# A hybrid RWKV-7 / S5 decoder layer on one core: the instruction order of the whole kernel made by the scheduler's other machine model

## The chip, the cores and the metric

The kernel runs on one core of one Trainium2 chip. The metric is the device time of one execution in microseconds (us), the median of several runs. Engines are named as in the profile: PE is the matrix engine (TensorE), DVE is VectorE, ACT is ScalarE, POOL is GpSimd, and SP is the engine that issues most of the DMA transfers. L172 means line 172 of the kernel. A "gap" of PE is time in which no matmul runs.

## What is computed

One layer of a decoder trunk, float32, 1024 tokens by 1024 channels. The reference, cut to its chain:

```
h = rms_norm(x) ; p = h @ w_in                  # columns: RWKV-7 r,k,v and low-rank parts | S5 input u | two gates
A = rwkv7_branch(p[rwkv columns])               # token shift, decay, delta-rule state, 8 heads of 64
B = s5_branch(p[S5 columns])                    # 32 groups, 64 complex states each, then GELU and a sigmoid GLU
m = sigmoid(gate_A) * (A @ w_A) + sigmoid(gate_B) * (B @ w_B)
x = x + rms_norm(m @ w_out)
z = rms_norm(x) @ w_up ; z = conv_b + sum(conv_w[j] * shift(z, 2 - j) for j in 0..2)
gate, val = split(z) ; x = x + rms_norm((gelu(gate) * val) @ w_down)
```

## The kernel before

**Tiling.** Activations are kept channel by token, in tiles of 128 channels by 512 tokens, so the 1024 tokens are two halves (`th` 0 and 1) and the 1024 channels are eight tiles (`k`). Each matrix product in float32 is made of three matmuls on a high and a low part of each operand: high times high, high times low, low times high (L172 to L174 in `mm3_steps`, L1049 to L1051 in `start`, L1614 to L1616 in `down`). Parts are made by a cast on ACT and a subtraction on DVE: L226/L227 (`split`) and L231/L232 (`split_half`) for activations, L156/L157 (`load_w`) for weights. A weight tile thus costs a load on SP's queue (`wf`, L155), a cast on ACT (`wh`, L156) and a subtraction on DVE (`wl`, L157), and DVE's part of it must be done before the third of its matmuls.

**Stages, in order of time.**

- `start` (L951 to L1061; the first 80 us). The columns of the S5 input, for token half 0 and then half 1. The loop runs over the eight `k`, and inside over four column blocks `b`, each with its own PSUM bank `gm`. Alongside, DVE adds up squares (L989, L991); `root` and `scales` make the norm's factors `rbc` with the reciprocal root `rsy` (L131 to L139). After the last `k` of half 0, `evict` (L1011 to L1020) empties each bank with one DVE multiplication, L1013. Half 1 starts in the same four banks, so its first matmul in bank `b` (L1049) waits for the L1013 of bank `b`. `scaled` (L1006 to L1009) multiplies the input tiles by `rbc` on DVE (L1008) and splits them (L226/L227) for all later products.
- `s5_setup` (from L311). DVE rows on 128x32 tiles, a chain that makes the coefficients of the S5 recurrence (sine, cosine, powers). They are needed by later stages only.
- The input projections of RWKV-7 (`rkv`, L1073 to L1077 make the token shift from the PSUM bank), `rwkv_prep` (L640 to L737: scans L672, products L691 to L696, L704, masks L720, shrinks L736), the inverse and state steps, `rwkv_out` (L901 to L939: norms over a head), the gates (L1147 empties a bank on ACT), the S5 branch (L1166/L1167 load a tile and apply GELU on ACT), L812 (block transposes of S5 data on DVE that the L822 matmuls read).
- The two branch projections and their merge (L1192, L1238, L1275, splits L232), `outproj`, and beside it `mid_norms(0)` for the first half of the tokens, with `post_norm` (L1295 scales, L1296 adds the residual, L259 sums squares).
- The MLP: `first_units` (four tiles of the up projection, convolution L1381/L1383 on DVE), `prep_t` (L1357 to L1368: differences and splits of eight tiles), then `fast_up` (a convolution with fewer products; `fast_weights`, L1408 to L1433, loads two weight tiles `r1` and `r2` of 128x1024 by L1420/L1421), and `down` with the last norm.

**What sets the order.** PE's order is written out: the program runs in a section whose PE order is manual (L1748), and `drive` and `background` (L185 to L223) interleave several generators into it. For DVE, ACT, POOL and SP a scheduler takes the instructions, their dependences and priorities, and a model of the machine, and makes one list for each engine before the kernel is run. Priorities are raised in places: weights (HPW and HPN, 400000 and 500000), the RWKV and norm lanes (HP, HP2, 100000 and 200000, L1932 and L1933). On the chip every engine works through its own list. The few lines of `start` that matter for the first 80 us:

```
for th in range(2):
    ps = [self.gmp() for b in range(4)]
    for k in range(NK):
        for b in range(4):
            ...
            nc.tensor.matmul(ps[b], a, hi, start=k == 0, stop=False)
            ...
            if k == NK - 1:
                evict(th, b, ps[b])
        ...
        if th:
            scaled(0, k)
```

## Time and profile before

| what | us |
|---|---|
| median of 3 runs (1488.82 to 1491.57) | 1489.53 |
| span of the profiled execution | 1491.1 |
| PE busy | 1435.8 |
| DVE busy | 1071.2 |
| ACT busy | 729.8 |
| POOL busy | 58.9 |

The profile is of one execution, whose span is 1.6 us above the median of the runs. Busy times are sums over the whole span; the waits and the order of time are in the views that the prediction shows. In rows of the timeline the columns are: start, duration, engine, line, operation, output and inputs, tile shape, count, and in brackets the idle time of the engine just before and what ended it. In rows of the windows the columns are: stretch, its length, then busy time and count for PE, PE's weight loads, DVE, ACT and POOL, the granted clock of PE (1.00 is full), the share of the DMA engines in use and GB/s.

### The profile page before, as it was taken

The page shows a single profiled execution, that of the slowest core. Times are in us where ns is not written, and L with a number is a line of the kernel's source. Part 1 is how long each engine was busy: PE and PEld are TensorE (multiplying, and loading weights), DVE is VectorE, ACT ScalarE, POOL GpSimd, SP SyncE. Part 2 cuts the span into 40 slices and gives each one's busy share as a digit, 9 for nine tenths or more (in the row PEclk, how much of TensorE's full clock was granted, in tenths as well). Part 3 has the DMA queues.
Part 4 walks back from the last instruction along what each step waited for, and adds up shares of the span by engine and source line. Part 5 has one row for each costly group of instructions (what it writes and reads, how often), then busy time and mean ns, then how long its engine had stood idle before and what let it go on. Part 6 is the DMA issues. An engine that isn't in the chain of part 4 may idle for free. (4 is left out here: it accounts for less than half of the span.)

```text
span 1491.1 us, 24155 instructions
## 1 busy us (share of the span) xinstructions
PE 1435.8 (96%) x9284; PEld 1176.3 (79%) x9284; DVE 1071.2 (72%) x1761; ACT 729.8 (49%) x1167; POOL 58.9 (4%) x116
## 2 busy tenths in 40 slices
PE   7999999999999989899999999999999999999996
PEld 5778888778878778677878877888888887888785
DVE  8977765665325859646597798777777777697677
ACT  7677653443324553633554455444444444443351
POOL 0000000010100110100000000000000000000001
PEclk9999999999999999899999999999999999999998
DMA  6453433633511575733374643222222227934723
GB/s 217 121 194 116 129 94 91 212 113 122 164 59 58 171 226 163 189 109 108 121 222 150 205 127 121 85 85 85 85 85 81 76 70 260 328 125 133 236 83 113
DMA packets 121284, 206.26 MB, mean 138 GB/s; under 512 B 29248, under 2 KB 35520, under 8 KB 121168
## 3 DMA queue, kind: packets, MB, share of 16 engines
q1 hardware_dynamic: 113296, 182.43, 39.2%
q0 software_dynamic: 6144, 19.99, 4.0%
q10 hardware_dynamic: 1728, 2.29, 0.4%
q8 instruction: 73, 1.20, 0.4%
q14 instruction: 43, 0.35, 0.1%
HBM read 150.14 MB, written 52.43 MB: 136 GB/s over the span
## 5 line engine op out<-in xcount | busy, mean ns | idle before, releaser
L172 PE MATMUL gm<-hh,wh 128*128 128x512 f32 x672 | 277.0, 412 | 10.5 <-DVE ev L1192 4.3
L173 PE MATMUL gm<-hl,wh 128*128 128x512 f32 x672 | 265.4, 395 | 0.0
L174 PE MATMUL gm<-hh,wl 128*128 128x512 f32 x672 | 265.2, 395 | 0.0
L156 ACT CAST wh<-wf 128x512 fp32r<-128x512 f32 x171 | 105.6, 619 | 168.3 <-PE gm L173 103.8
L157 DVE TENSOR_TENSOR wl<-wf,wh 128x512 fp32r<-128x512 f32 x171 | 116.9, 686 | 77.6 <-ACT wh L156 77.3
L172 PEld LDWEIGHTS gm<-hh,wh 128*128 128x128 f32 x672 | 127.6, 190 | 42.8 <-issue 5.9
L174 PEld LDWEIGHTS gm<-hh,wl 128*128 128x128 f32 x672 | 128.0, 190 | 28.1
L173 PEld LDWEIGHTS gm<-hl,wh 128*128 128x128 f32 x672 | 128.2, 191 | 24.7 <-issue 1.0
L1615 PE MATMUL d<-xl,wh 128*128 128x512 f32 x308 | 121.4, 394 | 3.5 <-DVE xl L227 3.5
L1614 PE MATMUL d<-xh,wh 128*128 128x512 f32 x308 | 121.4, 394 | 2.1 <-ACT xh L226 2.1
L1616 PE MATMUL d<-xh,wl 128*128 128x512 f32 x308 | 121.2, 393 | 0.0
L1440 PE MATMUL rp<-t,h 128*128 128x512 f32 x216 | 84.4, 391 | 1.6 <-ACT p L1454 1.6
L1442 PE MATMUL rp<-t,l 128*128 128x512 f32 x216 | 84.2, 390 | 0.5 <-DVE l L227 0.5
L1441 PE MATMUL rp<-t,h 128*128 128x512 f32 x216 | 84.1, 389 | 0.0
L1615 PEld LDWEIGHTS d<-xl,wh 128*128 128x128 f32 x308 | 58.6, 190 | 16.5 <-DVE xl L227 4.3
L1614 PEld LDWEIGHTS d<-xh,wh 128*128 128x128 f32 x308 | 58.5, 190 | 14.8 <-ACT xh L226 2.5
L1616 PEld LDWEIGHTS d<-xh,wl 128*128 128x128 f32 x308 | 58.6, 190 | 12.2
L226 ACT CAST h<-r 128x1024 fp32r<-128x1024 f32 x34 | 35.8, 1054 | 61.1 <-PE rp L1441 29.6
L227 DVE TENSOR_TENSOR l<-r,h 128x1024 fp32r<-128x1024 f32 x34 | 41.6, 1224 | 29.2 <-ACT h L226 27.7
L1461 DVE SCALAR_TENSOR_TENSOR y<-zv,vecs,y 128x1023 f32<-128x1023 f32 (+1 forms) x36 | 46.1, 1280 | 8.5 <-ACT y L1459 8.5
L1440 PEld LDWEIGHTS rp<-t,h 128*128 128x128 f32 x216 | 40.5, 188 | 11.2 <-ACT p L1454 2.5
L1454 ACT COPY p<-rp 128x512 f32<-128x512 f32 x54 | 31.0, 574 | 36.5 <-PE rp L1442 36.5
(459 smaller groups left out, 3199.4 us busy)
## 6 DMA issues: line engine op xcount, KB each, us to landing
r<-in_w_up_dram SPq DMA_DIRECT2D x36, 512.0 KB, 3.7
wf<-in_w_in_dram SPq DMA_DIRECT2D x62, 256.0 KB, 3.1
st<-in_w_down_dram SPq DMA_DIRECT2D x55, 256.0 KB, 4.1
st<-ACT SPq DMA_DIRECT2D x44, 256.0 KB, 4.5
wf<-in_w_up_dram SPq DMA_DIRECT2D x36, 256.0 KB, 2.9
ACT<-y POOLq DMA_DIRECT2D x18, 512.0 KB, 2.9
GT<-ev SPq DMA_DIRECT2D x32, 256.0 KB, 2.6
wf<-in_w_br_dram SPq DMA_DIRECT2D x32, 256.0 KB, 2.9
```

Source lines behind the costliest of these rows:

```text
L156: nc.scalar.copy(h[:, :n], f[:, :n])
L157: nc.vector.tensor_tensor(l[:, :n], f[:, :n], h[:, :n].bitcast(F32), ALU.subtract)
L172: mm(ps, a, xh[k], start=k == 0, stop=False)
L173: mm(ps, a, xl[k], start=False, stop=False)
L174: mm(ps, b, xh[k], start=False, stop=k == n - 1)
L1440: mm(ps, wh[:, c], xh, start=first and k == 0, stop=False, skip_group_check=True)
L1441: mm(ps, wh[:, c], xl, start=False, stop=False, skip_group_check=True)
L1442: mm(ps, wl[:, c], xh, start=False, stop=k == 3, skip_group_check=True)
L1461: V.scalar_tensor_tensor(y[:, lag:], z[:, 0:1024 - lag], self.vec(nme, i), y[:, lag:], ALU.mult, ALU.add)
L1614: mm(ps, wh[:, c], xh[:, x], start=start, stop=False, skip_group_check=True)
L1615: mm(ps, wh[:, c], xl[:, x], start=False, stop=False, skip_group_check=True)
L1616: mm(ps, wl[:, c], xh[:, x], start=False, stop=stop, skip_group_check=True)
```

## The change

One line of `build` opens a scheduling block around the whole kernel, with a flag that has the scheduler use its other machine model (a simulation of the timeline) when it makes the lists of the engines:

```
     def build(self):
         tc, nc = self.tc, self.nc
-        with tc.tile_pool(name="const", bufs=1) as self.const, tc.tile_pool(name="small", bufs=1) as self.small, \
+        with tc.block(schedule_with_timeline_sim=True), tc.tile_pool(name="const", bufs=1) as self.const, tc.tile_pool(name="small", bufs=1) as self.small, \
                 tc.tile_pool(name="dram", bufs=1, space=DRAM) as self.dram:
```

The instructions, their tiles and their counts stay the same on every engine, and so does the order of PE's 7448 instructions. What moves is the lists of the others: 1176 of DVE's 1761 rows (by up to 105 places later and 76 earlier), 495 of ACT's, 305 of SP's 688 transfers, 24 of POOL's. The numbers in tile names are higher by one after the change: `gm_346` before is `gm_347` after.

The first place is DVE's list in `start`. `ev` <- `gm` is the L1013 row that empties a bank, `x` the L1008 scaling, `sm`, `pw`, `s5q`, `s5ar` and `s5ai` the small rows of `s5_setup`. Before:

```order
76 L324 TENSOR_SCALAR sm_821<-sm_809 128x32
77 L1008 SCALAR_TENSOR_TENSOR x_198<-x_198,vecs,rbc_482 128x512
78 L1013 TENSOR_TENSOR ev_501<-gm_346,rbc_482 128x512
79 L991 TENSOR_TENSOR sq_540<-sq_540,sq_494 128x512
80 L1013 TENSOR_TENSOR ev_509<-gm_347,rbc_482 128x512
81 L227 TENSOR_TENSOR hl_562<-x_198,hh_561 128x512
82 L1013 TENSOR_TENSOR ev_517<-gm_348,rbc_482 128x512
83 L1008 SCALAR_TENSOR_TENSOR x_199<-x_199,vecs,rbc_482 128x512
84 L1008 SCALAR_TENSOR_TENSOR x_200<-x_200,vecs,rbc_482 128x512
85 L1013 TENSOR_TENSOR ev_525<-gm_349,rbc_482 128x512
```

The same engine after, around the first and the last of the four evictions:

```order
151 L331 TENSOR_TENSOR sm_970<-sm_928,sm_965 128x32
152 L1013 TENSOR_TENSOR ev_502<-gm_347,rbc_483 128x512
153 L1008 SCALAR_TENSOR_TENSOR x_199<-x_199,vecs,rbc_483 128x512
154 L1008 SCALAR_TENSOR_TENSOR x_200<-x_200,vecs,rbc_483 128x512
155 L1008 SCALAR_TENSOR_TENSOR x_201<-x_201,vecs,rbc_483 128x512
156 L1008 SCALAR_TENSOR_TENSOR x_202<-x_202,vecs,rbc_483 128x512
```

```order
184 L439 TENSOR_SCALAR s5w_988<-sm_974 64x32
185 L439 TENSOR_SCALAR s5w_991<-sm_974 64x32
186 L439 TENSOR_SCALAR s5w_988<-sm_980 64x32
187 L439 TENSOR_SCALAR s5w_991<-sm_980 64x32
188 L465 TENSOR_TENSOR s5ar<-pw_1016,pw_1017 128x64
189 L1013 TENSOR_TENSOR ev_526<-gm_350,rbc_483 128x512
```

The four evictions stood in rows 78, 80, 82 and 85, and stand in rows 152, 166, 181 and 189. Ahead of the fourth came 104 rows: 92 small ones, seven splits L227 and five scalings L1008.

The second place is DVE's list beside the output projection, where `hl` <- `et`, `hh` is the low half of a tile (L232) that PE reads next, `mx` are the rows of `post_norm` (L1295, L1296), and `tm` the sums of squares (L259). Before:

```order
1010 L232 SCALAR_TENSOR_TENSOR hl_8312<-et_8288,hh_8311 128x512
1011 L1192 SCALAR_TENSOR_TENSOR et_8342<-et_8342,ch_8350 128x512
1012 L157 TENSOR_TENSOR wl_8417<-wf_8418,wh_8416 128x512
1013 L1275 TENSOR_TENSOR et_8342<-et_8342,hl_7555 128x512
1014 L232 SCALAR_TENSOR_TENSOR hl_8339<-et_8315,hh_8338 128x512
1015 L259 TENSOR_TENSOR tm_8187<-tm_8187,tm_8182 128x512
1016 L232 SCALAR_TENSOR_TENSOR hl_8366<-et_8342,hh_8365 128x512
```

After:

```order
1029 L259 TENSOR_TENSOR tm_8206<-tm_8206,tm_8200 128x512
1030 L1192 SCALAR_TENSOR_TENSOR et_8343<-et_8343,ch_8351 128x512
1031 L259 TENSOR_TENSOR tm_8212<-tm_8212,tm_8206 128x512
1032 L1275 TENSOR_TENSOR et_8343<-et_8343,hl_7556 128x512
1033 L259 TENSOR_TENSOR tm_8218<-tm_8218,tm_8212 128x512
1034 L259 TENSOR_TENSOR tm_8224<-tm_8224,tm_8218 128x512
1035 L232 SCALAR_TENSOR_TENSOR hl_8367<-et_8343,hh_8366 128x512
```

The last of these splits (`hl_8366` before, `hl_8367` after) moved from row 1016 to row 1035. Ahead of it came six L1295, six L1296, six L259 and one L157.

The third place is SP's list before `fast_up`, where `wf` are weight tiles of 128x512 and `r` the tiles of 128x1024 of `fast_weights`. Before:

```order
455 L155 DMA wf_9666<-in_w_up_dram 128x512
456 L155 DMA wf_9672<-in_w_up_dram 128x512
457 L155 DMA wf_9737<-in_w_up_dram 128x512
458 L155 DMA wf_9743<-in_w_up_dram 128x512
459 L155 DMA wf_9783<-in_w_up_dram 128x512
460 L155 DMA wf_9789<-in_w_up_dram 128x512
461 L155 DMA wf_9821<-in_w_up_dram 128x512
462 L155 DMA wf_9827<-in_w_up_dram 128x512
463 L1420 DMA r_1865_9878<-in_w_up_dram 128x1024
464 L1421 DMA r_1866_9879<-in_w_up_dram 128x1024
465 L1420 DMA r_1876_9905<-in_w_up_dram 128x1024
```

After:

```order
443 L155 DMA wf_9667<-in_w_up_dram 128x512
444 L1420 DMA r_1865_9879<-in_w_up_dram 128x1024
445 L1421 DMA r_1866_9880<-in_w_up_dram 128x1024
446 L1420 DMA r_1876_9906<-in_w_up_dram 128x1024
447 L155 DMA wf_9673<-in_w_up_dram 128x512
448 L155 DMA wf_9738<-in_w_up_dram 128x512
449 L155 DMA wf_9744<-in_w_up_dram 128x512
450 L155 DMA wf_9784<-in_w_up_dram 128x512
451 L155 DMA wf_9790<-in_w_up_dram 128x512
452 L155 DMA wf_9822<-in_w_up_dram 128x512
```

Three `r` transfers moved ahead of seven `wf` transfers (six of them shown). On DVE in the same stretch the weight rows L157 stand up to 29 places later: ahead of the one that makes `wl` from `wf_9673` came eight L1365, eight L227, five L1381, six small L1383, one L1394 and one L1425.

More of the change, by code (lines that the diff above doesn't have):

```diff
@@ L1730, in build @@
         tc, nc = self.tc, self.nc
-        with tc.tile_pool(name="const", bufs=1) as self.const, tc.tile_pool(name="small", bufs=1) as self.small, \
+        with tc.block(schedule_with_timeline_sim=True), tc.tile_pool(name="const", bufs=1) as self.const, tc.tile_pool(name="small", bufs=1) as self.small, \
                 tc.tile_pool(name="dram", bufs=1, space=DRAM) as self.dram:
```

## The prediction

> **What bounds the kernel now.** I read the page first, then the waits of PE by what ended them, then the timeline at each place where the new lists differ and PE waits or comes close to it.

> ```profile
> span 1491.1 us, 24155 instructions
> PE 1435.8 (96%) x9284; PEld 1176.3 (79%) x9284; DVE 1071.2 (72%) x1761; ACT 729.8 (49%) x1167; POOL 58.9 (4%) x116
> ```

> PE is busy for 1435.8 of 1491.1 us. The change leaves its instructions and their order alone, so all that a better order of the others could win is PE's idle time, 1491.1 - 1435.8 = 55.3 us.

> ```profile
> PE gm L1049 <- ACT wh L226: 6.6, 1, 6.6
> PE gm L172 <- DVE ev L1192: 4.3, 2, 3.0
> PE gm L172 <- ACT ev L1147: 4.2, 2, 2.7
> ```

> Columns: who waits for whom, us in total, how often, the longest. The largest is the very first matmul waiting for its first weight (6.6), which no order of later work touches. The rest are waits of 1 to 3 us, spread over the span. There is little to win, and a lot to lose: wherever a row that PE needs soon is put behind rows that it needs late, PE gets a wait it doesn't have, and being nearly full it can't make it up later.

> **The change part by part.** The method is the same at each place: the rows that came ahead of a row, times the step from one such row to the next, is how much later that row ends; less the time by which it was early for PE. Each place is measured against PE's own clock, which by then is late by the sum of the places before.

> *Steps, and the start (20 to 80 us).*

> ```profile
> 50.80:57.20 6.40, 6.40 (x32) 5.31 (x31) 6.34 (x64) 1.81 (x8) 0.00 (x0) 1.00 0.16 56
> ```

> This stretch is almost only small `s5_setup` rows: 64 DVE rows in 6.34 us, 0.10 us a row.

> ```profile
> 38.88 0.69 DVE L1013 TENSOR_TENSOR ev<-gm,rbc 128x512 f32<-128x512 f32 x1
> 39.48 1.28 DVE L227 TENSOR_TENSOR hl<-x,hh 128x512 fp32r<-128x512 f32 x2
> 40.68 2.08 DVE L1008 SCALAR_TENSOR_TENSOR x<-x,vecs,rbc 128x512 f32<-128x512 f32 x3
> 42.67 1.89 DVE L227 TENSOR_TENSOR hl<-x,hh 128x512 fp32r<-128x512 f32 x3
> ```

> Two L227 take 40.68 - 39.48 = 1.20, so 0.60 a row; three L1008 take 42.67 - 40.68 = 1.99, so 0.66. Ahead of the fourth eviction came 92 small rows (9.2), seven L227 (4.2) and five L1008 (3.3): 16.7 us.

> ```profile
> 37.58 0.51 PE L1049 MATMUL gm<-hh,wh 128*128 128x512 f32 x1 [0.24 <-DVE ev L1013]
> ...
> 39.62 0.50 PE L1049 MATMUL gm<-hh,wh 128*128 128x512 f32 x1 [1.07 <-DVE ev L1013]
> ```

> PE already waits for that eviction (its bank's matmul is at 39.62), so the whole 16.7 us is added. The third eviction, which PE waits for at 37.58, has 85 small rows, seven L1008 and seven L227 ahead of it: 17.3, about the same. The first L1013 of the second half has 37 rows more ahead of it as well, 7.9 us; I put 3 of that on PE's path, as DVE can do the rest while it waits for the late PE. **+20** (17 to 22).

> ```profile
> 80.00:266.00 186.00, 186.00 (x1023) 159.31 (x1021) 125.91 (x180) 110.95 (x194) 5.46 (x18) 0.99 0.39 121
> ```

> From 80 to 266 us PE (second number) is busy for all of it, so none of the 20 is made up there.

> *RWKV preparation (266 to 300 us).*

> ```profile
> 283.16 0.69 DVE L692 TENSOR_TENSOR ar<-ld,gr 128x512 f32<-128x512 f32 x1 [1.81 <-DMA ld<-RKV]
> ...
> 294.55 2.39 DVE L672 TENSOR_TENSOR_SCAN ld<-csts,ld 128x512 f32<-128x512 f32 x2 [0.82 <-DMA ld<-TZ]
> ```

> ```profile
> 281.00 0.40 PE L172 MATMUL gm<-hh,wh 128*128 128x512 f32 x1
> ...
> 292.20 0.99 PE L716 MATMUL cz<-ar,bk 64*64 64x128 f32 x28
> ```

> Both L692, which wait for a load until 283.16, now stand ahead of the token shift L1073 that frees the bank of the matmul at 281.00: 283.16 + 1.2 + 0.9 for L1073 and L1077 = 285.3, 4.3 late. The two scans L672, waiting until 294.55, now stand ahead of the L704 whose result the matmul at 292.20 reads: 294.55 + 2.3 (scans) + 0.66 + 0.60 (two rows) + 0.7 = 298.8, 6.6 late, the 4.3 included. **+6** (4 to 8).

> *Masks (490 to 501 us).*

> ```profile
> 492.23 1.23 DVE L672 TENSOR_TENSOR_SCAN ld<-csts,ld 128x512 f32<-128x512 f32 x1 [0.56 <-DMA ld<-TZ]
> ```

> ```profile
> 491.61 1.98 PE L716 MATMUL cz<-ar,bk 64*64 64x128 f32 x64
> ...
> 500.86 2.29 PE L682 MATMUL rp<-csts,gr 128*128 128x2 f32 x15 [1.25 <-DVE ld L736]
> ```

> All four masks L720 now stand behind this scan, and the last also behind the second scan (1.15), four rows of 0.6 to 0.66, two L917 of 1.15 each and some small rows: 493.4 + 9 = 502.4, where the second part of the matmuls at 491.61 needs it at 492.5. That is 9.9, of which the wait of 1.25 at 500.86, no longer the last one there, gives some back. **+8** (4 to 10).

> *A gate's eviction (543 us).*

> ```profile
> 546.43 1.18 ACT L1167 ACTIVATE hh<-ld 128x512 f32<-128x512 f32 x1 [0.98 <-DMA ld<-YU]
> ```

> ```profile
> 543.95 0.50 PE L172 MATMUL gm<-hh,wh 128*128 128x512 f32 x1 [1.48 <-ACT ev L1147]
> ```

> The L1147 row that PE waits for now stands behind the GELU at 546.43, which waits for its load: 546.43 + 1.1 + 0.64 = 548.2, where it was done for the matmul at 543.95: 4.3 late. ACT's work is not more, so PE's next wait for it, 2.70 us at 557.34 (below), can take back up to that. **+3** (0 to 4).

> *Block transposes (619 us).*

> ```profile
> 617.93 1.43 DVE L812 STREAM_TRANSPOSE ld<-gr 32x512 f32<-32x512 f32 x2
> ...
> 623.26 0.69 DVE L232 SCALAR_TENSOR_TENSOR hl<-ev,hh 128x512 fp32r<-128x512 f32 x1
> ```

> ```profile
> 619.41 1.19 PE L822 MATMUL cz<-ld,gr 32*32 32x32 f32 x62 [0.29 <-DVE ld L812]
> 622.64 0.28 PE L822 MATMUL rp<-ld,gr 32*32 32x32 f32 x2 [2.03 <-ACT hh L231]
> ```

> The two pairs L812 now come after the L232 at 623.26: the first ends at 623.9 + 1.4 = 625.3, 5.9 late, the second 1.4 later; the wait of 2.03 before 622.64, which these also end, gives some back. **+4** (2 to 6).

> *Output projection (748 to 784 us).*

> ```profile
> 766.38 0.69 DVE L232 SCALAR_TENSOR_TENSOR hl<-et,hh 128x512 fp32r<-128x512 f32 x1
> ```

> ```profile
> 768.08 0.39 PE L173 MATMUL mm<-hl,wh 128*128 128x512 f32 x1
> ```

> ```profile
> 748.00:784.00 36.00, 35.72 (x160) 29.64 (x161) 35.53 (x59) 19.11 (x34) 1.08 (x2) 1.00 0.70 220
> ```

> Here DVE is busy 35.53 of 36 us. Ahead of this L232 came six L1295 of 0.66 and thirteen rows of 0.60: 11.8 us. It was 768.08 - 767.07 = 1.0 early. **+10** (6 to 11).

> *Before `fast_up` (850 to 915 us).*

> ```profile
> 891.58 0.68 DVE L157 TENSOR_TENSOR wl<-wf,wh 128x512 fp32r<-128x512 f32 x1
> ```

> ```profile
> 898.60 0.39 PE L174 MATMUL mm<-hh,wl 128*128 128x512 f32 x1
> ```

> ```profile
> 850.00:900.00 50.00, 49.34 (x219) 40.20 (x218) 47.86 (x86) 30.15 (x50) 2.16 (x4) 1.00 0.41 126
> ```

> Ahead of this L157 came 29 rows: seventeen of 0.60, six L1381 and L1425 of 0.6 to 0.66, six of 0.12: 14.7 us. It was 898.60 - 892.26 = 6.3 early, and DVE idles 50 - 47.86 = 2.1 before it: 14.7 - 8.4 = 6.3 late. SP's list does the same thing: the `r` transfers, which wait for a buffer that an L1365 row frees, hold seven weight loads behind them. That L1365 moved earlier too, so I add nothing, and up to 4 for the range. **+6** (4 to 12).

> *The other moved rows* (the small swaps in `fast_up` and `down` above all): I found no row there that comes later than PE uses it by more than 2 us. Taken at 0, with PE's slack as cover; 5 either way for the range.

> *The clock.*

> ```profile
> 557.34 0.79 PE L172 MATMUL gm<-hh,wh 128*128 128x512 f32 x1 [2.70 <-ACT ev L1147]
> ```

> ```profile
> 544.00:548.00 4.00, 4.00 (x18) 3.31 (x19) 0.00 (x0) 2.81 (x4) 0.57 (x1) 1.00 0.62 163
> 556.00:563.40 7.40, 6.06 (x14) 4.79 (x15) 5.96 (x15) 5.02 (x12) 0.00 (x0) 0.54 0.59 177
> ```

> Around the wait of 2.70 us the granted clock (third column from the right) is 0.54, so 6 us of matmuls take nearly twice as long: about 3 lost beside the wait itself. After the wait of 1.48 that ends at 543.95 it is 1.00, and nothing is lost. The change makes about five long waits where there were none; I price each at half of a loss between 2 and 3: **+6** (0 to 15). [...]

> **Sum:** 20 + 6 + 8 + 3 + 4 + 10 + 6 + 6 = 63. 1491.1 + 63 = 1554.1 for the profiled execution, whose span is 1.6 above the median: **1552.5**. Low ends: 17 + 4 + 4 + 0 + 2 + 6 + 4 + 0 - 5 = 32, 1521; high ends: 22 + 8 + 10 + 4 + 6 + 11 + 12 + 15 + 5 = 93, 1582.

> **The rivals.**

> *A late PE finds its data ready.* Several of my prices rest on loads that land at a fixed time (283.16, 294.55, 492.23, 546.43). If these are bound to SP and not to PE, they land early once PE is 20 us behind, and places two to five cost almost nothing. Then the start and the output projection remain, whose rows are pure DVE work: 20 + 10 = 30, 1520. Against it: the buffers into which they load are freed by rows that are late as well. 0.17.

> *The waits feed each other.* A late bank delays DVE's and ACT's rows that depend on it, and the small swaps in `fast_up` come to cost. With half as much again as my sum, 95: 1584, and up to 1620. For it: DVE is at 72% overall and at 96 to 99% in the two windows shown. 0.10.

> *Faster: the new lists remove waits.* The second and third row of the waits above (4.3 + 4.2 = 8.5 us), evictions that a list can put earlier, are what an order can win most directly; with the clock after them, about 11: 1478. This decides if the small rows put ahead of the first four evictions cost nothing, that is if the evictions end by 40 us as now. Against it: the step of 0.10 us a small row, and the row counts. 0.08.

> *No difference.* The lists do differ, so it would take gains and losses that cancel. 0.03.

> **How the numbers follow.** My forecast has the rest, 0.62. The range takes in the first rival and most of the bounds, 1508 to 1590. A measurement of this kernel can tell about 0.2%, 3 us, from no change. Faster 0.08, same 0.03, slower the rest, 0.89.

> **What would show it right or wrong.** In the profile after: PE's waits for L1013 go from 1.07 + 0.24 to some 18 us in the first 65 us, DVE is full from 30 to 60 us; new waits of PE for L1073 or L704, L720, L812, L232 and L157 of 4 to 10 us each; PE's busy time higher only by what the clock adds. Wrong would be: PE's idle time in the first 80 us not above 12 us; or new waits that end on lines I don't name; or a span under 1508.

## The result and the profile after

| | before | after |
|---|---|---|
| median, us (same chip) | 1490.31 (1488.82 to 1491.57, 4 runs) | 1567.43 (1559.39 to 1569.24, 4 runs) |
| span of the profiled execution | 1491.1 | 1565.4 |
| PE busy | 1435.8 | 1462.8 |
| PE idle (span less busy) | 55.3 | 102.6 |

The ratio is 1.0502, 95% interval 1.0474 to 1.053: slower by 77 us, where 63 were forecast. The time lies in the range.

The page of after, its span and its busy times:

```profile
span 1565.4 us, 24135 instructions
...
PE 1462.8 (93%) x9284; PEld 1190.9 (76%) x9284; DVE 1068.0 (68%) x1761; ACT 731.0 (47%) x1167; POOL 57.6 (4%) x116
```

The 74.3 us between the two spans are 47.3 us more of waiting (102.6 - 55.3) and 27.0 us more of PE being busy with the same 9284 matmuls. DVE, ACT and POOL have the work they had: it is order alone. The forecast had 57 of waits and 6 of clock, so the waits were put too high and the clock far too low.

PE's waits in after, by line and by what ended them (us in total, how often, the longest):

```profile
PE cz L822 <- DVE ld L812: 11.2, 2, 10.8
PE gm L1049 <- DVE ev L1013: 10.3, 2, 5.6
PE gm L1049 <- ACT wh L226: 6.7, 1, 6.7
PE d L1615 <- DVE xl L227: 6.1, 3, 4.9
PE cz L716 <- DVE gr L720: 5.8, 3, 3.5
PE gm L172 <- ACT ev L1147: 5.7, 2, 3.4
PE chk L245 <- DVE sq L991: 4.5, 1, 4.5
PE mm L173 <- DVE e L232: 4.1, 2, 3.4
```

Where before had waits of 1 to 3 us besides the one for the first weight, after has one of 10.8, two of 4.6 and 5.6 at the evictions, one of 4.9, one of 4.5. L1013, L720, L1147, L812 and L232 were named; L991 and the L227 of `down` were not. By the prediction's own signs the two unnamed ones, 4.5 and 4.9 us long, speak against it, and the waits for L1013 come to 12.8 us (10.3 here and one of 2.5 behind them) where it had some 18.

How late PE is, I read by one rule: the start of the same matmul in both traces, one from the other. PE's order is the same, so every matmul has its twin. At the borders of the places:

| between (us, before) | late at the end, us | added here | forecast |
|---|---|---|---|
| 0 and 80 (start) | +20.3 | 20 | 20 |
| 80 and 302 (token shift, preparation) | +20.6 | 0 | 6 |
| 302 and 490 | +26.0 | 5 | 0 |
| 490 and 518 (masks) | +31.6 | 6 | 8 |
| 518 and 563 (gate) | +30.9 | -1 | 3 |
| 563 and 616 | +28.0 | -3 | 0 |
| 616 and 631 (block transposes) | +39.9 | 12 | 4 |
| 631 and 744 | +40.2 | 0 | 0 |
| 744 and 769 (output projection) | +52.1 | 12 | 10 |
| 769 and 830 (norm beside `first_units`) | +61.7 | 10 | 0 |
| 830 and 916 (before `fast_up`) | +68.9 | 7 | 6 |
| 916 and 1425 | +66.6 | -2 | 0 |
| 1425 and 1428 (`down`) | +73.6 | 7 | 0 |

Here the clock is inside each place; the forecast had its 6 us apart. The rows behind the table, place by place.

The start. PE's timeline in after, with the idle time before each matmul in brackets:

```profile
28.66 1.84 PE L245 MATMUL chk<-ones,sq 128*128 128x1 f32 x8 [4.46 <-DVE sq L991]
...
47.60 0.80 PE L1049 MATMUL gm<-hh,wh 128*128 128x512 f32 x1 [5.64 <-DVE ev L1013]
53.88 0.80 PE L1049 MATMUL gm<-hh,wh 128*128 128x512 f32 x1 [4.63 <-DVE ev L1013]
```

And the first and the last of DVE's four evictions in after, which ran from 34 to 39.6 us before:

```profile
40.25 0.68 DVE L1013 TENSOR_TENSOR ev<-gm,rbc 128x512 f32<-128x512 f32 x1
...
54.70 0.68 DVE L1013 TENSOR_TENSOR ev<-gm,rbc 128x512 f32<-128x512 f32 x1
```

The last ends at 55.4 in place of 39.6: 15.8 later, for the 16.7 that the count of rows gave. A wait that I had not seen comes first: the sum of squares L991 for the norm stands behind other rows too, and makes PE 6.1 us late by 30 us.

The block transposes. DVE, POOL and PE in after: the last row of the matrix `mt`, its way to DRAM (`xd`) and back into `gr`, the transposes that read it, and the matmul:

```profile
646.88 0.22 DVE L791 TENSOR_TENSOR mt<-mt,tm 128x31 f32<-128x31 f32 x1
...
656.82 1.46 DVE L812 STREAM_TRANSPOSE ld<-gr 32x512 f32<-32x512 f32 x2 [4.97 <-DMA gr<-xd]
```

```profile
647.72 0.54 POOL L793 DMA_DIRECT2D xd<-mt  x1 [69.06 <-ACT hh L231]
654.34 1.98 POOL L798 DMA_DIRECT2D gr<-xd  x3 [6.08 <-DMA xd<-mt]
```

```profile
657.67 0.28 PE L822 MATMUL cz<-ld,gr 32*32 32x32 f32 x2 [10.76 <-DVE ld L812]
```

The last L791 before:

```profile
600.33 0.20 DVE L791 TENSOR_TENSOR mt<-mt,tm 128x31 f32<-128x31 f32 x1
```

Before, L812 started only at 617.93, 17.6 later: the round trip had room. In after the L791 is 46.5 us later, while PE is 28 late there, and L812 starts 9.9 us after it and has waited 4.97 for the transfer. So it isn't L812's place that binds, as the forecast said, but a chain on the same engine that feeds a transfer.

The other long waits, PE in after (masks; output projection; the norm; before `fast_up`; `down`):

```profile
523.93 0.68 PE L716 MATMUL cz<-ar,bk 64*64 64x128 f32 x2 [3.50 <-DVE gr L720]
808.37 0.79 PE L173 MATMUL mm<-e,wh 128*128 128x512 f32 x1 [3.38 <-DVE e L232]
879.80 1.67 PE L245 MATMUL rp<-ones,tm 128*128 128x1 f32 x8 [1.85 <-ACT tm L257]
944.95 0.79 PE L174 MATMUL ch<-hh,wl 128*128 128x512 f32 x1 [2.18 <-DVE wl L157]
1497.39 0.79 PE L1615 MATMUL d<-xl,wh 128*128 128x512 f32 x1 [4.94 <-DVE xl L227]
```

What stood ahead on DVE at the third and the fifth of them, in after:

```profile
872.52 5.36 DVE L1295 SCALAR_TENSOR_TENSOR mx<-mx,vecs,rp 128x512 f32<-128x512 f32 x8
...
1494.97 1.23 DVE L1569 TENSOR_TENSOR S<-st,S 128x1024 f32<-128x1024 f32 x1 [2.63 <-DMA st<-in_w_down_dram]
1496.12 1.22 DVE L227 TENSOR_TENSOR xl<-T,xh 128x1024 fp32r<-128x1024 f32 x1
```

The last pair is a swap of two neighbours. Before:

```profile
1423.98 1.22 DVE L227 TENSOR_TENSOR xl<-T,xh 128x1024 fp32r<-128x1024 f32 x1
1426.51 1.22 DVE L1569 TENSOR_TENSOR S<-st,S 128x1024 f32<-128x1024 f32 x1 [1.30 <-DMA st<-in_w_down_dram]
```

There the L1569 waited for its weights behind the L227. After, the L227 stands behind the L1569 and so behind its transfer: 4.94 us of waiting, 7.0 with the clock.

### The profile page after: what moved, and what is told of

Read it like the earlier page. It is cut to its first block, busy times and chain, and to the rows that moved or that the text cites. A ratio compares the mean times of both kernels' runs of the same rounds, so it can differ in the third digit from the quotient of the medians.

```text
span 1565.4 us, 24135 instructions
## 1 busy us (share of the span) xinstructions
PE 1462.8 (93%) x9284; PEld 1190.9 (76%) x9284; DVE 1068.0 (68%) x1761; ACT 731.0 (47%) x1167; POOL 57.6 (4%) x116
## 3 DMA queue, kind: packets, MB, share of 16 engines
q10 hardware_dynamic: 1728, 2.29, 0.4%
## 5 line engine op out<-in xcount | busy, mean ns | idle before, releaser
L172 PE MATMUL gm<-hh,wh 128*128 128x512 f32 x672 | 277.8, 413 | 13.5 <-ACT ev L1147 5.7
L173 PE MATMUL gm<-hl,wh 128*128 128x512 f32 x672 | 265.7, 395 | 0.0
L174 PE MATMUL gm<-hh,wl 128*128 128x512 f32 x672 | 265.7, 395 | 0.0
L157 DVE TENSOR_TENSOR wl<-wf,wh 128x512 fp32r<-128x512 f32 x171 | 116.8, 686 | 95.0 <-ACT wh L156 94.7
L172 PEld LDWEIGHTS gm<-hh,wh 128*128 128x128 f32 x672 | 128.2, 191 | 46.5 <-ACT ev L1147 6.5
L174 PEld LDWEIGHTS gm<-hh,wl 128*128 128x128 f32 x672 | 128.2, 191 | 28.3
L173 PEld LDWEIGHTS gm<-hl,wh 128*128 128x128 f32 x672 | 128.5, 191 | 24.8 <-issue 1.2
L1615 PEld LDWEIGHTS d<-xl,wh 128*128 128x128 f32 x308 | 58.3, 189 | 19.4 <-DVE xl L227 7.3
L226 ACT CAST h<-r 128x1024 fp32r<-128x1024 f32 x34 | 35.9, 1055 | 64.1 <-PE rp L1441 32.5
L227 DVE TENSOR_TENSOR l<-r,h 128x1024 fp32r<-128x1024 f32 x34 | 41.6, 1224 | 30.0 <-ACT h L226 28.5
L1440 PEld LDWEIGHTS rp<-t,h 128*128 128x128 f32 x216 | 40.8, 189 | 11.9 <-ACT p L1454 3.3
L1442 PEld LDWEIGHTS rp<-t,l 128*128 128x128 f32 x216 | 40.9, 189 | 8.5
```

The source lines that it names most:

```text
L157: nc.vector.tensor_tensor(l[:, :n], f[:, :n], h[:, :n].bitcast(F32), ALU.subtract)
L172: mm(ps, a, xh[k], start=k == 0, stop=False)
L173: mm(ps, a, xl[k], start=False, stop=False)
L174: mm(ps, b, xh[k], start=False, stop=k == n - 1)
L227: (eng or self.nc.vector).tensor_tensor(lo, x, hi.bitcast(F32), ALU.subtract)
L1440: mm(ps, wh[:, c], xh, start=first and k == 0, stop=False, skip_group_check=True)
```

## The experiments

Theory 1: each place where a DVE row that PE needs soon was put behind rows that it needs late costs what the prediction's method gives, a late PE does not change that much, and the costs add up; the clock comes on top. Rivals, by place: it is something else there (a transfer, the clock, or the lateness that PE brings).

All kernels but one are the kernel before plus a piece that pins the order of every list (DVE, ACT, SP, POOL), so that any mixture of the two kernels' lists can be run with the same instructions:

```
     with tile.TileContext(nc) as tc:
         Kern(tc, args, out).build()
+        _force(tc, nc)
...
+def _force(tc, nc):
+    by = {x.name: x for x in nc.all_instructions()}
+    info = mybir.DependencyInfo(mybir.DependencyClass.NoSync, mybir.DependencyReason.DATA)
+    for order in _ORDERS:
+        for p, n in zip(order, order[1:]):
+            tc.add_manual_dep(by[f"I-{n}"], f"I-{p}", info, reason="order")
```

The edges only order a list, and pinning by itself costs nothing that shows: in the first run below PE is 23.2 us late at 262 us, where the lists of before begin, and 22.9 at 537. What differs is `_ORDERS`, and the short diffs below show that. Ratios are to runs of before taken beside each kernel, with medians of 1486.7 to 1488.4, and 1490.31 beside after. Where a run is set against after, the two medians were not taken side by side; by the ratios such a gain comes out 5 us smaller, so it is known to about that.

**One place alone: the start.**

```
-_ORDERS = lists of before
+_ORDERS = lists of before, of after up to 262 us (309 DVE rows, 124 of ACT, 90 of SP, 4 of POOL stand elsewhere)
```

> The kernel before, with the lists of DVE, ACT, SP and POOL taken from the changed kernel for the first 262 us and left as before for the rest. Theory 1 (each place costs what its own list costs): matched matmul by matmul, the changed kernel is 20.1 us later than the kernel before at 80 us and 21 at 262, so this kernel takes 1490 + 20 = 1510 (1507 to 1513), with the same two waits of PE for L1013 of 5 to 6 us each. Theory 2 (a late PE finds its data ready, so later stages take part of a delay back): 1495 to 1504. Theory 3 (one delay sets off others further on): over 1516.

Measured: 1512.8 (1508.32 to 1513.91), ratio 1.0171 (1.0139 to 1.0202), 25 us. In its trace PE is 22.8 us late at 80 us, and still 19.4 at the end. The start costs by itself what after loses in its first 80 us, and PE makes up no more than 3.4 of it.

**One place alone: 537 to 640 us.**

```
-_ORDERS = lists of before
+_ORDERS = lists of before, of after at 537 to 640 us (118 DVE rows, 44 of ACT, 15 of SP, 5 of POOL stand elsewhere)
```

> The kernel before, with the lists of the changed kernel from 537 to 640 us only (GELU, the gate's evictions, the glu and branch products, the block transposes L812). Theory 1: in the changed kernel PE's lateness goes from 31.7 us at 530 to 39.9 at 631, made of about -3 up to 616 and +10.8 at the first L822 matmul, so this kernel takes 1490 + 8 = 1498 (1495 to 1501), with one wait of PE for L812 of about 10 us. Theory 2 (the 10.8 us come from the start being late): no such wait, 1487 to 1492.

Measured: 1499.61 (1497.53 to 1500.86), ratio 1.0087 (1.0064 to 1.011), 13 us. PE in this run:

```profile
626.23 0.28 PE L822 MATMUL cz<-ld,gr 32*32 32x32 f32 x2 [10.73 <-DVE ld L812]
```

The wait is as long as in after (10.76), though PE is not late here when it comes to this place. So it isn't brought by what came before.

**One place alone: 745 to 790 us.**

```
-_ORDERS = lists of before
+_ORDERS = lists of before, of after at 745 to 790 us (58 DVE rows, 38 of ACT, 20 of SP stand elsewhere)
```

> The kernel before, with the lists of the changed kernel from 745 to 790 us only (output projection beside the first post norm). Theory 1: lateness went from 39.9 to 51.7 us there, so 1490 + 11.8 = 1502 (1499 to 1505), of which PE's idle time is about 7 and the halved clock after the waits the rest. Theory 2 (the price is DVE's rows alone, 10 us as predicted, and the clock loses nothing): 1500, with idle time of 10.

Measured: 1500.7 (1497.88 to 1501.25), ratio 1.0092 (1.0069 to 1.0115), 14 us; in its trace PE loses 11.7 between 744 and 769, 11.9 in after.

**One place alone: 790 to 850 us**, where the forecast had nothing and after loses 10.

```
-_ORDERS = lists of before
+_ORDERS = lists of before, of after at 790 to 850 us (66 DVE rows, and rows of ACT and SP, stand elsewhere)
```

> The kernel before, with the lists of DVE, ACT, SP and POOL taken from after only where before works at 790 to 850 us (post_norm beside first_units and the splits behind it), a place that the prediction had at nothing, and where after loses 10 us. Theory 1 (these lists themselves cost it: rows of post_norm ahead of the rows that PE waits for): +8, against 1486.7 of the kernel before 1495 (1491 to 1500), and most of it between 790 and 850 us in the trace. Rival (the 10 us are what the earlier places do here, DVE and ACT being late for a late PE): within 3 us of before, 1488 (1485 to 1490).

Measured: 1496.38 (1490.8 to 1501.79), ratio 1.0063 (1.0038 to 1.0088), 6 to 13 us. PE waits there for rows that `post_norm` held up:

```profile
809.71 1.07 PE L245 MATMUL rp<-ones,t 128*128 128x1 f32 x8 [1.22 <-DVE t L1323]
...
825.11 1.05 PE L245 MATMUL rp<-ones,tm 128*128 128x1 f32 x8 [1.98 <-ACT tm L257]
```

In the profiled execution the place takes 4.7 us, half of what it takes in after. The waits are the same: these two are 3.2 us together, and 3.1 in after. What differs is the clock, which is halved for 3.4 us at this place here and for 13.6 in after. The place is real and was overlooked; about 3 of its 10 us are waits, and by my estimate nearly 7, half of the 13.6, are the clock, whose part is not the same in every execution.

**Undone in after: the first four evictions.** This kernel is the one after, with edges that put the 104 DVE rows behind the fourth L1013 again; the scheduler places the rest.

```
+_FIRST = 528          # the fourth L1013
+_LATER = [825, 827, ...]   # 104 rows
+    for n in _LATER:
+        tc.add_manual_dep(by[f"I-{n}"], f"I-{_FIRST}", info, reason="order")
```

> The changed kernel, with one constraint more: the 104 DVE rows that came ahead of the fourth eviction L1013 of the start must stand behind it again; the scheduler orders the rest as before with its other machine model. Theory 1: the start's 20 us go away, clock included, and the rest stays: 1567 - 20 = 1547 (1543 to 1551). Theory 2 (what the late start cost is needed again later, as loads and other rows are no longer hidden behind it): 1555 or more. Theory 3 (one delay sets off others): below 1540.

Measured: 1547.64 (1538.04 to 1550.32), ratio 1.0400 to before (1.036 to 1.044), 20 less than after. The total is as expected, the way is not. PE in this run:

```profile
27.90 1.84 PE L245 MATMUL chk<-ones,sq 128*128 128x1 f32 x8 [5.00 <-DVE sq L991]
...
42.12 0.50 PE L1049 MATMUL gm<-hh,wh 128*128 128x512 f32 x1 [0.56 <-DVE ev L1013]
...
69.21 0.76 PE L172 MATMUL gm<-hh,wh 128*128 128x512 f32 x1 [2.94 <-DVE ev L1013]
```

The evictions no longer hold PE up at 42 us. But the wait for L991 stays, and a new one comes with the evictions of the second half, so that at 80 us only 11 of the 20 are won. The rest is won at 420 to 530 us: the wait of 2.17 that after has at 427 us is gone, and the longest one for the masks is 2.05 in place of 3.50. The scheduler's lists of this kernel differ from those of after in the start, at 519 to 553 us and at 882 to 899 as well. So the 20 that were expected came out partly by luck; the next run, with pinned lists, is the clean test of the start as a whole.

**Undone in after: the whole start.**

```
-_ORDERS = lists of after
+_ORDERS = lists of after, of before up to 262 us (309 DVE rows, 124 of ACT, 90 of SP, 4 of POOL back)
```

> The kernel after the change, with the lists of all engines in the first 262 us taken from before (the start with its evictions and s5_setup, the first second). Theory 1 (the places' costs add up: the start alone cost 25): 1567 - 25 = 1542 (1538 to 1546). Rival A (a PE that is late anyway hides part of the later places, so they cost more once the start is whole): 1552 (1547 to 1558). Rival B (the late start makes the later places dearer): below 1537.

Measured: 1539.67 (1535.48 to 1543.2), ratio 1.0356 (1.0327 to 1.0385), 27.8 less than after, against 25 for the start alone. Rival A, in which a late PE hides the later places, is not what came, and rival B's line is not reached. The later places together cost with a punctual PE what they cost with one that is 20 us late: 52.1 us from 262 us to the end, against 53.3 in after. Single places differ by up to 6, the gate above all (4.6 here, -1 in after); the wait at the L822 is 9.95, and the output projection costs 11.6.

**Undone in after: L789/L791 alone.**

```
 L1192, L1238, L157, L232 ... (DVE rows of the branch projections)
-L789, L791 (tile mt) between and behind them
+L789, L791 (tile mt) ahead of those that passed them
 L232, L812, L812
```

> The kernel after the change, with the 60 rows L789/L791 of the second S5 matrix (tile mt) put back ahead of the DVE rows that pass them; the four L812 stay behind the second L232, as after. Theory 1 (the 10.8 us of the first L822 come from the round trip: mt to DRAM and back into gr, which begins when the last L791 ends): mt ends some 18 us earlier, the blocks land before the L232 rows are done, and the wait of the first L822 falls from 10.8 to about 5, what L812's own place behind L232 costs: 1562 (1558 to 1565). Rival (the place of L812 behind L232 is the whole cost, as the prediction had it): the wait stays near 10.8 and the time near 1567 (1564 to 1570).

Measured: 1567.26 (1566.74 to 1569.23), no gain. DVE and POOL in this run, and PE:

```profile
637.63 0.20 DVE L791 TENSOR_TENSOR mt<-mt,tm 128x31 f32<-128x31 f32 x1
...
662.80 2.89 DVE L812 STREAM_TRANSPOSE ld<-gr 32x512 f32<-32x512 f32 x4
```

```profile
644.11 0.73 PE L172 MATMUL gm<-hh,wh 128*128 128x512 f32 x1 [2.64 <-DVE ev L1192]
650.09 0.47 PE L172 MATMUL gm<-hh,wh 128*128 128x512 f32 x1 [0.96 <-DVE ev L1192]
655.14 0.47 PE L172 MATMUL gm<-hh,wh 128*128 128x512 f32 x1 [2.08 <-DVE ev L1192]
663.64 0.28 PE L822 MATMUL cz<-ld,gr 32*32 32x32 f32 x2 [5.81 <-DVE ld L812]
```

Theory 1 is half right. `mt` ends 9.3 us earlier (18 were expected), L812 waits for no transfer any more (no bracket), and the L822 wait falls to 5.81. That is about what the forecast's step has for L812's place behind L232, 5.9 before anything is given back. But the rows that were put back pushed L1192, L1238 and the loads behind them, and PE waits there instead.

**Undone in after: L812 alone.**

```
+L812 STREAM_TRANSPOSE ld<-gr 32x512 x2
 L232 ... hl<-ev,hh 128x512
 L1192, L227, L1238
+L812 STREAM_TRANSPOSE ld<-gr 32x512 x2
 L232 ... hl<-ev,hh 128x512
-L812 STREAM_TRANSPOSE ld<-gr 32x512 x2
-L812 STREAM_TRANSPOSE ld<-gr 32x512 x2
```

> The kernel after the change, with only the four L812 put back ahead of the two L232 that they stood ahead of before; the rows L789/L791 stay late. Theory 1 (round trip): the blocks still land at about the same time, the first L822 still waits 10 us or so, and now the splits L232 stand behind the waiting L812 too: no gain, 1567 to 1575, 1569. Rival (the place of L812 is the cost): 5 to 6 us less, 1562 (1559 to 1565).

Measured: 1565.71 (1564.6 to 1567.69), within 2 us of after. DVE and PE in this run:

```profile
659.44 1.43 DVE L812 STREAM_TRANSPOSE ld<-gr 32x512 f32<-32x512 f32 x2 [8.95 <-DMA gr<-xd]
```

```profile
660.28 0.28 PE L822 MATMUL cz<-ld,gr 32*32 32x32 f32 x2 [9.98 <-DVE ld L812]
```

With L812 first DVE stands still for 8.95 us, waiting for the transfer, and PE for 9.98. The rival, L812's place as the whole cost, is out.

**Undone in after: the whole of 537 to 640 us.**

```
-_ORDERS = lists of after
+_ORDERS = lists of after, of before at 537 to 640 us (118 DVE rows, 44 of ACT, 15 of SP, 5 of POOL back)
```

> The kernel after the change, with the lists of all engines taken from before only where before works at 537 to 640 us (118 DVE rows, 44 of ACT, 15 of SP, 5 of POOL stand elsewhere than after). Putting single rows back there (L812 alone, or the L789/L791 alone) gave nothing. Theory 1 (the place is one knot of rows on a full DVE, and costs some 10 us that come back only with the whole of it): 1557 (1553 to 1560), the 10.8 us of the first L822 gone and not replaced. Rival (a PE that is 28 us late meets other loads and buffers there, so that also the rows of before cost it): above 1562.

Measured: 1556.13 (1552.45 to 1556.89), ratio 1.046 (1.0437 to 1.0483), 11 less than after. PE in this run:

```profile
648.93 0.22 PE L822 MATMUL cz<-ld,gr 32*32 32x32 f32 x2 [0.29 <-ACT hh L231]
```

The wait of 10.76 is gone, and nothing replaces it: PE is 33.4 us late at 537 us and 30.1 at 616. I read the three runs as chains that lie over each other, L791 to the transfer, L812 behind L232, and L1192 to the banks, on an engine with little room: DVE is busy for 37.21 of the 42 us from 605 to 647 in after. Shown is that single rows put back give nothing and the whole place gives the 11; which smaller set would do, no run shows.

**Undone in after: the four places together.**

```
-_ORDERS = lists of after
+_ORDERS = lists of after, of before up to 262, at 537 to 640, 745 to 790 and 790 to 850 us
```

> The kernel after the change, with the lists of before at the four places that were tried alone: up to 262, 537 to 640, 745 to 790 and 790 to 850 us. Theory 1 (costs add up: 28 for the start undone, 10, 12 and 9 for the others): 1567 - 59 = 1508 (1503 to 1513), that is 21 above the kernel before, for the masks, the place before fast_up, the last L227 and the small ones. Rival (each place makes the next one dearer, as a late PE makes DVE rows late): below 1500.

Measured: 1509.0 (1506.04 to 1509.98), ratio 1.0145 (1.0123 to 1.0167), 58.4 less than after. The sum was 59. What is left, 17 us in its trace, is where after has it: 5 between 302 and 563 us (9.5 by the end of the masks, of which 4 are given back), 7 before `fast_up` and 7 at the L227 of 1425 us, with steps of +3 and -5 between.

**Can a list beat both?** Nine rows of before moved by hand, each ahead of a row that is needed later:

```
+L226 lx<-ev                      (ACT, 75 us)
 L156 wh<-wf ; L1072 ev<-gm
-L226 lx<-ev
...
+L1147 ev<-gm                     (ACT, 557 us; another at 543)
 L756, L754, L767, L783, L756, L226, L156
-L1147 ev<-gm
...
+L227 xl<-st,xh                   (DVE, 1390 us; another at 1398)
 L1569 st<-A,st ; L227 wl<-st,wh
-L227 xl<-st,xh
```

> The kernel before, with nine rows moved by hand ahead of rows that are needed later: ACT's split of lx at 75 us and DVE's beside it; the two L1147 at 543 and 557 ahead of the GELU and of copies (PE waits 1.48 and 2.70 for them); L926 at 516 ahead of copies (2.19); one L232 at 601, which lets the GT load start for which PE waits 3.04 at 607; L1459 at 1252 behind the splits (2.06); two L227 of down ahead of the rows that wait for weights (1.21 and 2.26). Theory 1 (a place in a list is worth the wait that it ends, and the half-clock windows behind it): about 11 us of waits and 4 to 8 of clock, 1486 - 13 = 1473 (1466 to 1478). Rival (the waits come back at the next row, as at the L822): 1483 to 1488.

Measured: 1485.78 (1484.13 to 1491.79) against 1487.84, ratio 1.0001 (0.9985 to 1.0018): no difference. The waits that were aimed at did shrink, but two larger ones stand in their place. PE in this run, and DVE at the second:

```profile
556.38 0.80 PE L172 MATMUL gm<-hh,wh 128*128 128x512 f32 x1 [3.38 <-DVE hl L1192]
...
1251.72 0.69 PE L1614 MATMUL d<-xh,wh 128*128 128x512 f32 x1 [4.04 <-DVE zg L1470]
```

```profile
1249.69 1.28 DVE L1461 SCALAR_TENSOR_TENSOR y<-zv,vecs,y 128x1023 f32<-128x1023 f32 x1 [1.91 <-ACT y L1459]
1250.89 0.68 DVE L1470 TENSOR_TENSOR zg<-p,mm 128x512 f32<-128x512 f32 x1
```

At 1254 us I had moved ACT's L1459 back, because PE's wait was put down to ACT's split. But L1470, which empties a bank, stands on DVE behind the L1461 that reads what L1459 makes, so the later L1459 held PE up longer than the split had (4.04 for 2.06).

**The same with these two mended**, and one L157:

```
+L1470 zg<-p,mm                   (DVE, 1252 us)
 L1461 y<-zv,vecs,y
-L1470 zg<-p,mm
...
+L1192 hl<-ev,gm                  (DVE, 556 us)
 L227, L789, L791, L789
-L1192 hl<-ev,gm
...
-L157 wl<-wf,wh                   (DVE, 514 us)
 L696 ; L704
+L157 wl<-wf,wh
```

> The kernel of by_hand with three DVE rows moved as well, those that PE waited for in its trace instead: L1470 ahead of the L1461 that waits for ACT (PE waited 4.04 for it at 1252), L1192 ahead of a split and three L789/L791 (3.38 at 556), and one L157 behind an L704 (1.92 at 514). Theory 1 (by_hand gained at five places and lost at two, and a repair of these shows the gain): 6 us of waits and 2 to 4 of clock less than by_hand in one execution, 1478 (1474 to 1482). Rival (in this part of the program DVE and ACT have no room, and each wait that is ended comes back at the next bank): 1483 to 1488, the same as before.

Measured: 1481.69 (1476.87 to 1483.32) against 1488.38, ratio 0.9946 (0.9929 to 0.9964): 0.5% faster than before, a version that beats both. It is at the upper edge of what was expected, since the wait for L1192 shrank only from 3.38 to 2.89. Between the two profiled executions, this one and that of before, PE's busy time is 6.8 us shorter and its waiting 4.0, and the stretches at half clock are 17.1 us in place of 34.1: most of this gain is the clock, not the waits themselves.

## Why the prediction was right, and where it wasn't

**What bound the kernel** was read rightly: PE was 96% busy, there was little to win and a lot to lose, and the loss is PE's waits for rows that were put too late, with the clock behind them. The total is nearer than its parts: by the table some places came out 33 us above the forecast together, others 17 below, and its 6 us of clock lie inside the places, so that 11 us remain. That the total came so near is in part luck.

**The start (20 forecast, 20 in the trace, 25 alone).** Right in size. The method, rows ahead times the step of a row, gave 16.7 for the fourth eviction and the trace has 15.8. But the forecast hung all of it on L1013, and a second chain lies under it: the L991 alone makes PE 6 us late, so that the run with only the evictions repaired wins 11 there and not 20.

**Token shift and preparation (6, 0 in the trace).** This step failed. The rows L692 and L672 were taken to wait for loads that land when they land before. In after the L692, which waited 1.81 for its load before, waits for nothing, and PE has no wait between 290 and 325 us. The first rival would have it that PE's lateness helps, but it doesn't: in the run with the whole start undone PE comes to this place 2.2 us early, its lists are those of after, and it loses nothing there either (1.9 early at 302 us). What the forecast left out is that SP's list is new too, and starts these loads earlier. SP before, and SP and DVE in that run:

```profile
277.38 2.34 SPq L653 DMA_DIRECT2D ld<-RKV  x4
```

```profile
270.20 2.55 SPq L653 DMA_DIRECT2D ld<-RKV  x4
```

```profile
277.27 1.28 DVE L692 TENSOR_TENSOR ar<-ld,gr 128x512 f32<-128x512 f32 x2
```

The loads start 7.2 us earlier, of which PE's being early explains 2, and the L692 runs without a wait at 277.27, where it ran at 283.16. So the row stands ahead of the token shift, as forecast, but no longer holds it up.

**The gate's eviction (3, -1).** The wait came as forecast: PE waits up to 3.4 us for L1147 there, where it was 1.48. But the next wait for it is shorter, as foreseen, and the half-clock stretch that before has at 557 us does not come, so that nothing is left of it. That is one execution: in the run with the start undone the same lists bring a wait of 4.52 there, two stretches at half clock, and a cost of 4.6.

**Masks (8, 6), output projection (10, 12), before `fast_up` (6, 7).** Right in place and about right in size.

**Block transposes (4, 12).** The place was right and the cause was not. L812's place behind L232 leaves a wait of about the forecast's size (5.81) once `mt` is early, but in after it is hidden behind the later end of L789/L791 and its way through DRAM, which I had not followed: the rows of that chain stand 18 places later, scattered, and I had read only the rows next to the one that PE waits for.

**The other rows (0; 10 at 769 to 830, 5 at 302 to 490, 7 at 1425).** This was the largest hole: 22 us were put at nothing. At 769 to 830 eight L1295 in a row, and the L1296 behind them, hold up what the norm's matmuls read; that place costs by itself, 4.7 us in one execution and 10 in another with the same waits. At 1425 two neighbours changed places, and the one that came first waits for a transfer: a row's price is not its duration but its wait. At 302 to 490 PE has a wait of 2.17 that nothing in the profile ends; its cause stays open.

**The clock (6, 27 of PE's busy time).** Mis-sized by 21 us, more than the whole miss of the forecast, while the waits came out 10 lower than its 57. The forecast counted five long waits; after has fifteen stretches at half clock between 20 us after the start and 20 before the end, 102.4 us in all, where before has seven, 34.1 us. PE is idle for part of these 68 us more. It is busy in 48 of them, and half of that, some 24 us, is what the clock adds by this estimate (in after 9 matmuls of 128x512 fill a window of 3.41 us at half clock from 1497.85, and 16 the next one at full clock); the other 3 of the 27.0 I can't place.

**The rivals.** "A late PE finds its data ready" held nowhere that the runs can tell: the place that cost nothing costs nothing with a punctual PE either. "The waits feed each other" did not hold: 25 + 13 + 14 + 10 alone are 62, and undone together they give 58.4 (53 by the ratios), no more than their sum. "Faster" rested on waits that a list can end. Those exist, as the last run shows, but this scheduler's model did not find them.

## What to carry to other kernels

When one engine is full and a scheduler makes the lists of the others, read the new order from the full engine's side: for each row that it waits for, count what came ahead, and follow the chain behind that row back through its transfers, since the row that moved may stand far from the one that is waited for. When the list of the engine that issues the transfers is remade too, a landing time read before the change no longer holds. A row that itself waits for a transfer is priced at that wait, even in a swap of two neighbours. Where a second engine has little room, as DVE here, which was busy for 89% of such a stretch, single rows put right can give nothing, as another chain is late next; look in the next trace for the wait that took its place, and mend the two together.

## What the runs showed of the hardware

```profile
572.85:576.26 3.41, 1.62 (x8) 1.00 (x6) 0.55 (x1) 3.10 (x3) 1.84 (x4) 1.00 1.14 272
576.26:579.67 3.41, 1.78 (x8) 1.47 (x9) 0.26 (x1) 3.41 (x6) 0.54 (x1) 1.00 0.70 245
579.67:583.09 3.42, 3.42 (x21) 2.93 (x20) 2.46 (x5) 2.76 (x6) 0.00 (x0) 1.00 0.81 264
```

```profile
1491.02:1494.44 3.42, 1.43 (x7) 0.85 (x5) 1.32 (x2) 2.29 (x3) 0.00 (x0) 1.00 0.58 155
1494.44:1497.85 3.41, 0.46 (x1) 0.47 (x2) 2.88 (x3) 0.00 (x0) 0.00 (x0) 0.50 0.01 2
1497.85:1501.26 3.41, 3.41 (x9) 2.64 (x9) 3.41 (x4) 0.00 (x0) 0.00 (x0) 0.50 0.60 191
```

The first wait falls half into each of two windows, each is busy for about half (1.62 and 1.78 of 3.41), and the clock stays at 1.00. The second leaves 1.43 (42%) in one window and 0.46 in the next; the clock is 0.50 in the two windows that follow the first, and the second of them has 9 matmuls where the next one, at full clock, has 16. I counted the windows of these two profiles so, from 20 us after the start to 20 us before the end, PE's busy time being the union of its matmul records. Of those at full clock, the next one was at half in 10 of 10 when PE was busy under 40%, in 7 of 9 at 40 to 50%, in 2 of 6 at 50 to 60%, and in 3 of 802 above. After a window at half clock the next one was at full in 22 of 29 when PE was busy for 80% or more of it, and in 0 of 11 below that. By these counts, and as an estimate for this kernel alone, a wait of 2 us that lies within one window (busy for 41%) is mostly followed by a window at half clock, some 1.7 us more (half of 3.41), and the same wait split evenly by a border (busy for 71% in both) hardly ever is. No run moved a wait on the grid and left its length as it was.

The grid lay differently in the two executions: counted back from the changes, its first border is 0.25 us after the start of the span in before and 2.82 in after. This may be part of why single runs of before spread from 1480.78 (mean granted clock 0.989) to 1491.57 (one of 1491.1 has 0.983), which was not tried. The three windows above 60% that half clock followed, from 498.60 and 618.06 in before (busy for 2.17 and 2.25 of 3.42) and from 862.98 in after (2.14 of 3.41), hold matmuls of 128x2, of 64x64 and 32x32, and of 128x1; whether that is why, no run shows. The last of them holds a wait of only 1.27 us, which ends at 864.53, where the one of 3.42 us above left the clock at 1.00.
